# Ten instead of nine gate/up groups of a SwiGLU half-step as seven products of halves

## The chip, the cores and the metric

One core of one Trainium2 chip runs the whole program as a single launch. The metric is the device time in microseconds (us), the median of several runs. TensorE is written PE, its weight loads PEld, VectorE DVE, ScalarE ACT, GpSimd POOL, and SyncE, which issues nearly all transfers, SP.

## What is computed

The reference is one layer of a decoder trunk in float32, on 16 learned meta tokens and 256 tokens of width 2048:

```
h = h + 0.5 * (silu(norm(h) @ w_gate1) * (norm(h) @ w_up1)) @ w_down1        # D_FF = 5632
h = h + mixer(norm(h))            # w_in (2048 x 10248), two attentions, sigmoid gates, w_out
h = h + 0.5 * (silu(norm(h) @ w_gate2) * (norm(h) @ w_up2)) @ w_down2        # D_FF = 5632
return h[:, 16:]
```

## The kernel before

**Units.** Every weight matrix is cut into tiles of 128 x 1024 numbers (512 KB). One tile is a unit: SP loads it (`load`, tile `raw`), ACT rounds it to the faster format (`wh`), DVE takes the rest (`wl = raw - wh`, both in `split_unit`), and PE multiplies with both halves. There are three buffers each of `wh` and `wl`, so the split of a unit waits until PE is done with the unit three before it, and five buffers of `raw` (eight in the second half-step). `ahead(u)` runs ahead of `products(u)`: it issues the load of unit u+5 (u+8 in the second half-step) and the split of unit u+2. The order in which rows stand on an engine is that of the code, moved a little by a scheduler at build time.

**Plain units of the second half-step** multiply both halves of 128 tokens with one tile: 12 products of 512 columns (two halves of the tokens, two rows of 128 weights, and hi*hi, hi*lo, lo*hi). A gate/up pair of 512 features is two blocks of 8 units, 192 products.

**Seven products.** For the groups in `SEVENS` (`Group`) the gate and the up projection of 512 features are taken together as one product of two-by-two blocks with seven instead of eight block products (p1 to p7, Winograd's form). One of the seven takes 4 units of 6 products, so a group has 28 units and 168 products. The order in a group is p1 x4, p5 x4, (p6, p2, p4) x4, p3 x4, p7 x4. p1, p2, p3 read weights, p5, p6, p7 read sums of weights, and p4 reads p6's tile less p2's, which DVE works out (L1135). When the four units of one product are done its bank is evacuated: p1, p5, p6, p4 by an ACT copy, p2 by a DVE add and a silu, p3 by two DVE operations (L1028, L1029), p7 by DVE, silu on ACT and two more on DVE (L1033, L1035, L1036). Then `turn` transposes the result for the down product: eight PE transposes (L440), two ACT copies and two DVE differences.

**Sums of weights.** They don't depend on the tokens. `weight_sums` works them out early, beside the first half-step: for one quarter of a group three loads (tiles `pre`, nine buffers), three DVE subtractions (L1056 to L1060), three stores to DRAM (`sum`). `ahead` takes one of its steps with a pace of 0.94 a unit, from unit 20 to two units before the mixer. The `pre` tiles lie in a pool that `open_attention` closes, at the mixer's first block, and the attention's constants then lie in its place.

**What lies between.** A seven-product unit gives PE half the work of a plain one but costs ACT and DVE the same. So plain units are put between: `eight` holds the units of plain group 1 (16) and of the down projection (88, in parts `PART` of 4 tiles times n each), and ten of them go into every group.

**Mixer.** Its first blocks are q (8 units), forget (2), k (8), v (8) for four heads. PSUM has eight banks; a block of the mixer takes four.

Of the kernel before, what the change touches and what calls it, by code (L numbers as in the profile page):

```python
# [11 lines left out]
ALU = mybir.AluOpType  # L12
# [6 lines left out]
KT = D // P  # L19
# [33 lines left out]
def hybrid_layer(ctx: ExitStack, tc: tile.TileContext, x, meta_tokens, ffn1_norm, ffn1_w_gate, ffn1_w_up,  # L53
# [772 lines left out]

    for g in range(2):
        blocks.append(Block(wi, 0, KT, g * 512, 512, mrhs, NR, fox_evac("q", 4 * g)))
        if g == 0:
            blocks[-1].before = open_attention  # L830
            blocks.append(Block(wi, 0, KT, 3072, 128, mrhs, NT, ev_forget, stacked=8))
        blocks.append(Block(wi, 0, KT, 1024 + g * 512, 512, mrhs, NT, fox_evac("k", 4 * g)))
        blocks.append(Block(wi, 0, KT, 2048 + g * 512, 512, mrhs, NT, fox_evac("v", 4 * g)))
    for c in range(4):
        blocks.append(Block(wi, 0, KT, 6152 + c * 512, 512, mrhs, NR, gate_evac("f", c), True))
# [16 lines left out]

    SEVENS = (2, 3, 4, 5, 6, 7, 8, 9, 10)
    PART = (3, 2, 2, 2, 1, 1)
    acc = {}
    forms = {}

# [10 lines left out]
    def normal_forms():  # L870

        r = norms["ffn2"].r
        yield from residual_by_token()
        yield 1
        for c in range(4):
            for j in range(4):
                t = resid(4 * c + j)[:, :NR]
                act.activation(t, t, AF.Copy, scale=gcol[:, 32 + 4 * c + j:33 + 4 * c + j])
            for j in range(0, 4, 2):
                t = res[c][:, j:j + 2, :NR]  # L880
                dve.tensor_tensor(t, t, r[:, :NR].unsqueeze(1).to_broadcast([P, 2, NR]), op=ALU.mult)
                yield 1

        def x(i, k, c):

            return res[2 * k + c][:, :, i * P:(i + 1) * P]

        def pool():
            return fslot if len(forms) < 4 else slot

        def plain(n, i, k):
            f = pool()
            hi, lo = forms[n] = f([P, 8, P], F32R), f([P, 8, P], F32R)
            for c in range(2):
                split(hi[:, 4 * c:4 * c + 4, :], lo[:, 4 * c:4 * c + 4, :], x(i, k, c))
                yield 2

        def summed(n, t, a, b, op):

            f = pool()  # L900
            hi, lo = forms[n] = f([P, 8, P], F32R), f([P, 8, P], F32R)
            for c in range(2):
                cs = slice(4 * c, 4 * c + 4)
                dve.tensor_tensor(t[:, cs, :], a(c), b(c), op=op)
                yield 1
                split(hi[:, cs, :], lo[:, cs, :], t[:, cs, :])
                yield 2

        yield from plain("a11", 0, 0)
        t = slot([P, 8, P], F32)  # L910
        tq = lambda c: t[:, 4 * c:4 * c + 4, :]
        yield from summed("s1", t, lambda c: x(1, 0, c), lambda c: x(1, 1, c), ALU.add)
        yield from summed("s2", t, tq, lambda c: x(0, 0, c), ALU.subtract)
        yield from plain("a12", 0, 1)
        yield from plain("a22", 1, 1)
        yield from summed("s4", t, lambda c: x(0, 1, c), tq, ALU.subtract)
        t3 = slot([P, 8, P], F32)
        yield from summed("s3", t3, lambda c: x(0, 0, c), lambda c: x(1, 0, c), ALU.subtract)
        while not free["g0"]:
            yield 1  # L920
        yield from plain("a21", 1, 0)

    free = {"g0": False}

    def fslot(shape, dt):
        return ptile(shape, dt, "f", F_BUFS)
# [10 lines left out]

    hs2 = {}

    def plain_group(g):  # L940

        u = {}
        factor = lambda i: norms["ffn2"].rtok[:, i:i + 1] if g == 0 else 1.0

        def ev_gate(i, ps):
            if i == 0:
                u["t"] = slot([P, 2, 512], F32)
            assert norms["ffn2"].done
            act.activation(u["t"][:, i, :], ps[:], AF.Silu, scale=factor(i))

        def ev_up(i, ps):
            s = u["t"][:, i, :]
            if g == 0:
                dve.scalar_tensor_tensor(s, ps[:], factor(i), s, op0=ALU.mult, op1=ALU.mult)
                free["g0"] = i == 1
            else:
                dve.tensor_tensor(s, ps[:], s, op=ALU.mult)
            if i == 1:
                lanes["turn"].append(turn(u["t"], hs2, 4 * g))

        def rhs(kt):
            if g == 0:
                return norms["ffn2"].rhs(kt)
            return [[forms[f"a{i + 1}{kt // 8 + 1}"][m][:, kt % 8, :] for i in range(2)] for m in range(2)]

        return [Block(w[0], 0, KT, g * 512, 512, rhs, NR, ev, True)
                for w, ev in ((ffn2_w_gate, ev_gate), (ffn2_w_up, ev_up))]

    def down_blocks(t0, count, last):
# [120 lines left out]
    units = units_of(blocks)  # L1090
    second = len(units)
    mixer = next(u for u, (b, _, _) in enumerate(units) if b.w is wi)
    units += units_of(plain_group(0))
    seven = [(groups[g], p, u) for g in sorted(groups) for p, u in Group.ORDER]
    starts = [4 * sum(PART[:i]) for i in range(len(PART))]
    down = [down_blocks(t0, 4 * n, t0 + 4 * n == FT) for t0, n in zip(starts, PART)]
    eight = [plain_group(1), *down]
    eight = [u for bs in eight for u in units_of(bs)]
    for g, p, u in seven:
        units.append((g, p, u))  # L1100
        if p == "p2" or p in ("p5", "p3") and u % 2 or p in ("p1", "p7") and u == 1:
            units.append(eight.pop(0))
    units += eight
    raws, halves, banks, newest = {}, {}, {}, []
# [63 lines left out]
    def products(u):  # L1168
# [12 lines left out]
        for j in range(outs):  # L1181
# [10 lines left out]
            for i in range(0 if wide else n):  # L1192
                x = b.rhs(k0 + i)
                first, last = k0 + i == 0, k0 + i == b.kts - 1
                if b.by_token:
                    xh, xl = (x[0][j], x[1][j]) if isinstance(x, list) else (x[:, 0, cs], x[:, 1, cs])
                    terms = ((ps[:], xh, wh[:, i, :]), (ps[:], xh, wl[:, i, :]), (ps[:], xl, wh[:, i, :]))
                elif b.stacked:
                    terms = tuple((ps[:, :b.n], wh[:, i, cs], x[:, m, :b.n]) for m in range(2))
                else:  # L1200
                    o, xh, xl = ps[:, :b.n], x[:, 0, :b.n], x[:, 1, :b.n]
                    terms = ((o, wh[:, i, cs], xh), (o, wh[:, i, cs], xl), (o, wl[:, i, cs], xh))
                for m, (o, a, c) in enumerate(terms):
                    pe.matmul(o, a, c, start=first and m == 0, stop=last and m == len(terms) - 1)  # L1204
# [24 lines left out]

    def ahead(u):  # L1230
        nonlocal loaded, done, sums_due
        if SUMS_FROM <= u < mixer - 2:
            sums_due += SUMS_PACE
            while sums_due >= 1:
                sums_due -= 1
                next(ahead_sums, None)
        while loaded < min(len(units), u + (LOAD_AHEAD if u < second else SECOND_AHEAD)):
            load(loaded)
            loaded += 1
        while done < min(len(units), u + 1 + SPLIT_AHEAD):  # L1240
            split_unit(done)
            done += 1
# [69 lines left out]
```

## Time and profile before

| | |
|---|---|
| median of three runs | 2206.59 us (2205.45 to 2206.94) |
| profiled execution | 2207.63 us, span from first to last instruction 2205.9 us |
| PE busy | 2199.1 us, 13716 products and transposes |
| DVE busy | 1603.0 us, 73% of the span |
| ACT busy | 1170.5 us, 53% of the span |
| moved by DMA | 554.09 MB, mean 251 GB/s |

The profiled execution lies 1.04 us over the median of the runs and 1.7 us over its own span. Busy time of PE includes pipelined matmuls, whose ends are modelled, so idle time is better read from the starts of matmuls.

### The profile page before, as it was taken

To read this page: it belongs to the slowest core of one execution; us is meant where nothing else is said; L and a number is where in the kernel's file an instruction comes from. 1 tells how busy PE (TensorE), PEld (TensorE's weight loads), DVE (VectorE), ACT (ScalarE), POOL (GpSimd) and SP (SyncE) were. 2 spreads that over 40 slices of the span, in tenths; PEclk is the share of its full clock that TensorE was granted. 3 is DMA by queue.
4 is the path that set the end of the run, shared out by engine and by line. 5 is a ranking of instruction groups with operands and counts; after the bars stand their busy time and mean duration, and the time that the engine had idled before them with its cause. 6 is when DMAs were issued, how large, how long until landed. Compare 5 with 4: busy or idle time off the path is not lost.

```text
span 2205.9 us, 34841 instructions
## 1 busy us (share of the span) xinstructions
PE 2199.1 (100%) x13716; PEld 1997.0 (91%) x13716; DVE 1603.0 (73%) x1944; ACT 1170.5 (53%) x1467; POOL 42.1 (2%) x113
## 2 busy tenths in 40 slices
PE   9999999999999999999999999999999999999999
PEld 9999999999999999998899988888888888888887
DVE  6676666667766765889556665667888888888886
ACT  6344433334443454656445565458666666666663
POOL 0000000000000001110000000000000000000000
PEclk9999999999999999999999999999999999999999
DMA  7899999999999966555655456555788777888774
GB/s 225 281 330 324 340 318 348 343 338 333 347 336 340 323 202 191 164 166 158 190 183 164 146 156 201 179 187 163 241 272 269 261 262 260 275 272 270 258 260 171
DMA packets 262021, 554.09 MB, mean 251 GB/s; under 512 B 17289, under 2 KB 22241, under 8 KB 261857
## 3 DMA queue, kind: packets, MB, share of 16 engines
q1 hardware_dynamic: 259776, 548.34, 75.2%
q8 instruction: 107, 1.75, 0.3%
q10 hardware_dynamic: 1472, 2.37, 0.3%
q0 software_dynamic: 608, 1.16, 0.2%
q14 instruction: 58, 0.47, 0.1%
HBM read 493.07 MB, written 58.73 MB: 250 GB/s over the span
## 4 chain that ended last, share of the span: by engine, by line
PE 99%; DMA 0%; DVE 0%; SPq 0%; issue 0%; DVEq 0%; ACT 0%
PE acc L1204 72%; PE acc L1003 16%; PE acc L1187 5%; PE acc L1190 3%; PE aux L727 1%; PE aux L600 1%; PE aux L440 1%; PE aux L588 0%; PE aux L698 0%; DMA v<-in_meta_tokens_dram 0%; PE acc L1165 0%; PE aux L866 0%; PE aux L340 0%; PE aux L677 0%; PE aux L678 0%; PE aux L640 0%
## 5 line engine op out<-in xcount | busy, mean ns | idle before, releaser
L190 ACT ACTIVATE wh<-raw 128x1024 fp32r<-128x1024 f32 (+1 forms) x609 | 644.4, 1059 | 779.1 <-PE acc L1204 621.9
L191 DVE TENSOR_TENSOR wl<-raw,wh 128x1024 fp32r<-128x1024 f32 (+1 forms) x609 | 743.1, 1222 | 432.3 <-ACT wh L190 428.3
L1204 PE MATMUL acc<-v,wh 128*128 128x272 f32 x5264 | 991.4, 288 | 0.0
L1204 PEld LDWEIGHTS acc<-v,wh 128*128 128x128 f32 x5264 | 827.4, 189 | 0.1
L1204 PE MATMUL acc<-v,wl 128*128 128x272 f32 x2616 | 753.5, 289 | 0.4 <-DVE wl L191 0.4
L1204 PE MATMUL acc<-wh,v 128*128 128x512 f32 x1664 | 540.8, 392 | 0.0
L1204 PEld LDWEIGHTS acc<-v,wl 128*128 128x128 f32 x2616 | 490.8, 188 | 0.8 <-DVE wl L191 0.6
L1204 PEld LDWEIGHTS acc<-wh,v 128*128 128x128 f32 x1664 | 312.5, 188 | 64.6
L1136 DVE TENSOR_TENSOR wl<-raw,wh 128x1024 fp32r<-128x1024 f32 x252 | 305.1, 1221 | 41.5 <-ACT wh L1130 33.4
L1130 ACT ACTIVATE wh<-raw 128x1024 fp32r<-128x1024 f32 x252 | 266.5, 1060 | 124.3 <-PE acc L1204 75.4
L1204 PE MATMUL acc<-wl,v 128*128 128x512 f32 x832 | 327.8, 394 | 0.0
L1204 PEld LDWEIGHTS acc<-wl,v 128*128 128x128 f32 x832 | 156.2, 188 | 38.8 <-DVE wl L191 7.1
L1003 PE MATMUL acc<-wh,f 128*128 128x512 f32 x576 | 191.3, 393 | 0.0
L1187 PE MATMUL acc<-v,wh 128*128 128x512 f32 x512 | 160.6, 395 | 0.0
L1003 PE MATMUL acc<-wh,v 128*128 128x512 f32 x432 | 143.3, 389 | 0.0
L1003 PEld LDWEIGHTS acc<-wh,f 128*128 128x128 f32 x576 | 108.2, 188 | 22.5
L1190 PEld LDWEIGHTS acc<-v,wl 128*128 128x128 f32 x512 | 96.1, 188 | 22.0
L1003 PE MATMUL acc<-wl,f 128*128 128x512 f32 x288 | 113.2, 393 | 0.0
L1190 PE MATMUL acc<-v,wl 128*128 128x256 f32 x512 | 101.3, 279 | 0.0
L1003 PEld LDWEIGHTS acc<-wh,v 128*128 128x128 f32 x432 | 81.1, 188 | 16.9
L1003 PE MATMUL acc<-wl,v 128*128 128x512 f32 x216 | 84.0, 389 | 0.0
L1187 PEld LDWEIGHTS acc<-v,wh 128*128 128x128 f32 x512 | 78.4, 188 | 0.2
(264 smaller groups left out, 1378.5 us busy)
## 6 DMA issues: line engine op xcount, KB each, us to landing
raw<-in_ffn_w_down_dram SPq DMA_DIRECT2D x176, 512.0 KB, 5.4
raw<-in_ffn_w_gate_dram SPq DMA_DIRECT2D x175, 512.0 KB, 5.2
raw<-in_w_in_dram SPq DMA_DIRECT2D x162, 512.0 KB, 3.7
raw<-in_ffn_w_up_dram SPq DMA_DIRECT2D x140, 512.0 KB, 5.1
sum<-pre SPq DMA_DIRECT2D x108, 512.0 KB, 6.5
raw<-sum SPq DMA_DIRECT2D x108, 512.0 KB, 4.6
pre<-in_ffn_w_up_dram SPq DMA_DIRECT2D x72, 512.0 KB, 6.9
pre<-in_ffn_w_gate_dram SPq DMA_DIRECT2D x36, 512.0 KB, 6.8
```

Source lines behind the costliest of these rows:

```text
L190: act.activation(hi, src, AF.Copy)
L191: dve.tensor_tensor(lo, src, hi.bitcast(F32), op=ALU.subtract)
L440: pe.transpose(p[:, (2 * j + i) * P:(2 * j + i + 1) * P], u[:, i, c:c + P], ident[:])
L600: pe.matmul(po[:, :NR], a[:, ks], b[:, i * NR:(i + 1) * NR], start=n == 0, stop=n == 6)
L727: pe.matmul(o, a, b, start=start, stop=stop, skip_group_check=True)
L1003: pe.matmul(ps[:], a[:, kt, :], b[:, i, :], start=fresh and kt == 0 and m == 0, stop=kt == 7 and m == 2, skip_group_check=True)
L1130: act.activation(wh[:], raw[:], AF.Copy)
L1136: dve.tensor_tensor(wl[:], raw[:], wh[:].bitcast(F32), op=ALU.subtract)
L1187: pe.matmul(ps[:].rearrange("p (a t) -> p a t", a=2), wh[:, i, cs], x[:, :, :NR], start=k0 + i == 0, stop=False, skip_group_check=True)
L1190: pe.matmul(ps[:, :NR], wl[:, i, cs], x[:, 0, :NR], start=False, stop=k0 + i == b.kts - 1, skip_group_check=True)
L1204: pe.matmul(o, a, c, start=first and m == 0, stop=last and m == len(terms) - 1)
```

## The change

Gate/up group 1, until now computed as eight products between the others' units, becomes the first of ten groups by seven products. `plain_group(1)` and the form of the tokens that only it needed (`a21`) go; only group 0 stays plain (`first_group`). Its twelve more sums of weights need 24 more steps of `weight_sums`, 12 loads and 12 stores: the steps go on at 1.5 a unit into the mixer's first 15 units, and the forget block, which opens the attention, moves behind q and k. With 88 instead of 104 plain units to put between, groups 1 and 2 get four each (after p2), groups 3 to 9 eight (after p2, and after every second unit of p5 and p3), group 10 twelve. The down projection is cut into seven parts instead of six.

```
-        if g == 0:
-            blocks[-1].before = open_attention
-            blocks.append(Block(wi, 0, KT, 3072, 128, mrhs, NT, ev_forget, stacked=8))
-        blocks.append(Block(wi, 0, KT, 1024 + g * 512, 512, mrhs, NT, fox_evac("k", 4 * g)))
+        blocks.append(Block(wi, 0, KT, 1024 + g * 512, 512, mrhs, NT, fox_evac("k", 4 * g)))
+        if g == 0:
+            blocks.append(Block(wi, 0, KT, 3072, 128, mrhs, NT, ev_forget, stacked=8, before=open_attention))
...
-    SEVENS = (2, 3, 4, 5, 6, 7, 8, 9, 10)
-    PART = (3, 2, 2, 2, 1, 1)
+    SEVENS = (1, 2, 3, 4, 5, 6, 7, 8, 9, 10)
+    PART = (1, 2, 2, 2, 2, 1, 1)
...
-        while not free["g0"]:
-            yield 1
-        yield from plain("a21", 1, 0)
...
-        if p == "p2" or p in ("p5", "p3") and u % 2 or p in ("p1", "p7") and u == 1:
+        if p == "p2" or u % 2 and (g.g > 2 and p in ("p5", "p3") or g.g == SEVENS[-1] and p in ("p1", "p7")):
             units.append(eight.pop(0))
...
-        if SUMS_FROM <= u < mixer - 2:
-            sums_due += SUMS_PACE
+        if SUMS_FROM <= u < mixer + 15:
+            sums_due += SUMS_PACE if u < mixer - 2 else 1.5
```

How the change moves instructions is shown at three places. First DVE where one group ends and the next begins (after L1033, which is L1019 in the changed file: the evacuation of p7). Before, the rows are these; the L191 rows are splits of plain units, the L1136 rows those of seven-product units:

```order
L191 TENSOR_TENSOR wl_2868_18479<-raw_2846_18386,wh_2867_18478 128x1024
L1136 TENSOR_TENSOR wl_2871_18491<-raw_2849_18398,wh_2870_18490 128x1024
L1136 TENSOR_TENSOR wl_2874_18503<-raw_2852_18410,wh_2873_18502 128x1024
L1136 TENSOR_TENSOR wl_2877_18521<-raw_2855_18430,wh_2876_18520 128x1024
L1136 TENSOR_TENSOR wl_2880_18533<-raw_2858_18442,wh_2879_18532 128x1024
L1033 TENSOR_TENSOR v_2775_18067<-acc_2760_17998,v_2775_18067 128x512
L1035 TENSOR_TENSOR v_2776_18068<-v_2776_18068,acc_2760_17998 128x512
L191 TENSOR_TENSOR wl_2883_18549<-raw_2861_18456,wh_2882_18548 128x1024
L1036 TENSOR_TENSOR v_2776_18068<-v_2776_18068,v_2775_18067 128x512
L1136 TENSOR_TENSOR wl_2887_18562<-raw_2866_18476,wh_2886_18561 128x1024
```

In the changed kernel the same place (end of group 3, start of group 4; L1121 is the split of a seven-product unit) reads:

```order
L1121 TENSOR_TENSOR wl_2839_18300<-raw_2819_18209,wh_2838_18299 128x1024
L1121 TENSOR_TENSOR wl_2842_18312<-raw_2822_18221,wh_2841_18311 128x1024
L1121 TENSOR_TENSOR wl_2845_18324<-raw_2825_18239,wh_2844_18323 128x1024
L1019 TENSOR_TENSOR v_2741_17868<-acc_2731_17825,v_2741_17868 128x512
L1021 TENSOR_TENSOR v_2742_17869<-v_2742_17869,acc_2731_17825 128x512
L1121 TENSOR_TENSOR wl_2848_18340<-raw_2828_18251,wh_2847_18339 128x1024
L1022 TENSOR_TENSOR v_2742_17869<-v_2742_17869,v_2741_17868 128x512
L1121 TENSOR_TENSOR wl_2852_18353<-raw_2831_18265,wh_2851_18352 128x1024
```

The split behind the two evacuations was that of a plain unit, and is now that of the third unit of p1.

Second, DVE in group 1 of the changed kernel, from the last unit of p5 (`wl_2538`) over p6 and p2 to the first plain unit between and p4 (L1120 is p6's tile less p2's; the two rows on `aux` are the `turn` of group 0):

```order
L1121 TENSOR_TENSOR wl_2538_17001<-raw_2513_16907,wh_2537_17000 128x1024
L191 TENSOR_TENSOR v_2535_16995<-aux_2534_16990,v_2535_16995 128x2x256
L1121 TENSOR_TENSOR wl_2541_17013<-raw_2516_16927,wh_2540_17012 128x1024
L1121 TENSOR_TENSOR wl_2545_17031<-raw_2520_16940,wh_2544_17030 128x1024
L191 TENSOR_TENSOR v_2543_17027<-aux_2542_17022,v_2543_17027 128x2x256
L1120 TENSOR_TENSOR raw_2516_16927<-raw_2516_16927,raw_2520_16940 128x1024
L191 TENSOR_TENSOR wl_2548_17045<-raw_2523_16952,wh_2547_17044 128x1024
L1121 TENSOR_TENSOR wl_2551_17057<-raw_2516_16927,wh_2550_17056 128x1024
```

Before, two plain units stood between p5's units and one between p1's, so a turn's two differences came in three units' more time.

Third, SP at the mixer's first blocks (the tiles of `w_in`). Before, from the last store of a sum, it reads:

```order
L1052 DMA sum10_2_3_9135<-pre_1132_8789 128x1024
L1121 DMA raw_1173_9137<-in_ffn1_w_down_dram 128x2x512
L1121 DMA raw_1176_9167<-in_ffn1_w_down_dram 128x2x512
L1121 DMA raw_1179_9197<-in_ffn1_w_down_dram 128x2x512
L1121 DMA raw_1182_9227<-in_w_in_dram 128x2x512
L1121 DMA raw_1185_9257<-in_w_in_dram 128x2x512
```

and goes on with loads of `w_in` alone. In the changed kernel, from the fifth load of `w_in` on:

```order
L1106 DMA raw_1197_9339<-in_w_in_dram 128x2x512
L1057 DMA pre_1200_9369<-in_ffn2_w_gate_dram 128x2x512
L1057 DMA pre_1201_9371<-in_ffn2_w_up_dram 128x2x512
L1106 DMA raw_1202_9374<-in_w_in_dram 128x2x512
L1057 DMA pre_1211_9430<-in_ffn2_w_up_dram 128x2x512
L1106 DMA raw_1212_9433<-in_w_in_dram 128x2x512
L1038 DMA sum10_0_1_9459<-pre_1179_9174 128x1024
L1038 DMA sum10_1_1_9461<-pre_1183_9206 128x1024
L1106 DMA raw_1219_9463<-in_w_in_dram 128x2x512
L1038 DMA sum10_2_1_9485<-pre_1187_9239 128x1024
L1106 DMA raw_1222_9488<-in_w_in_dram 128x2x512
```

Between one load of `w_in` and the next there are now one or two transfers of the sums, up to the sixteenth load.

## Rows read from the trace of the kernel before

**Rows 1.** The page: busy time by engine, granted clock in 40 slices.
```profile
PE 2199.1 (100%) x13716; PEld 1997.0 (91%) x13716; DVE 1603.0 (73%) x1944; ACT 1170.5 (53%) x1467; POOL 42.1 (2%) x113
...
PEclk9999999999999999999999999999999999999999
```
**Rows 2.** Waits of PE, then PEld: us in total, times, longest us.
```profile
PE acc L1204 <- DVE wl L191: 0.4, 1, 0.4
...
PEld acc L1204 <- DVE wl L191: 9.4, 29, 0.6
```
**Rows 3.** The chain that ended last, in order of time: start us, us, what.
```profile
1758.16 5.44 PE acc L1003 x24
...
1825.19 5.44 PE acc L1003 x24
```
**Rows 4.** Windows: busy us (instructions) by engine, granted clock, DMA share, GB/s.
```profile
705.00:745.00 40.00, 40.00 (x321) 40.00 (x320) 26.40 (x30) 17.13 (x22) 0.00 (x0) 1.00 0.98 355
797.00:846.00 49.00, 49.00 (x343) 46.28 (x342) 32.88 (x60) 27.36 (x40) 3.52 (x13) 1.00 0.62 184
...
1771.50:1838.50 67.00, 67.00 (x298) 54.46 (x297) 57.21 (x55) 43.81 (x47) 0.00 (x0) 1.00 0.80 267
```
**Rows 5.** DVE groups by line, 1771.5 to 1838.5 us: busy us, mean ns.
```profile
L1136 DVE TENSOR_TENSOR wl<-raw,wh 128x1024 fp32r<-128x1024 f32 x28 | 33.9, 1221 | 3.9 <-ACT wh L1130 3.0
...
L1135 DVE TENSOR_TENSOR raw<-raw,raw 128x1024 f32<-128x1024 f32 x4 | 4.9, 1222 | 0.1
L933 DVE SCALAR_TENSOR_TENSOR v<-acc,v 128x512 f32<-128x512 f32 x4 | 2.6, 681 | 0.0
```
**Rows 6.** Timeline of DVE, ACT and PE where a group ends: start us, us.
```profile
1826.32 2.59 DVE L1136 TENSOR_TENSOR wl<-raw,wh 128x1024 fp32r<-128x1024 f32 x2 [0.30 <-ACT wh L1130]
1828.83 0.68 DVE L1033 TENSOR_TENSOR v<-acc,v 128x512 f32<-128x512 f32 x1
1829.42 0.68 DVE L1035 TENSOR_TENSOR v<-v,acc 128x512 f32<-128x512 f32 x1
1830.02 1.22 DVE L191 TENSOR_TENSOR wl<-raw,wh 128x1024 fp32r<-128x1024 f32 x1
1831.16 0.68 DVE L1036 TENSOR_TENSOR v<-v,v 128x512 f32<-128x512 f32 x1
...
1838.84 1.23 DVE L191 TENSOR_TENSOR wl<-raw,wh 128x1024 fp32r<-128x1024 f32 x1 [0.26 <-ACT wh L190]
...
1826.59 1.06 ACT L1130 ACTIVATE wh<-raw 128x1024 fp32r<-128x1024 f32 x1 [0.30 <-PE acc L1003]
...
1827.75 0.39 PE L1003 MATMUL acc<-wh,f 128*128 128x512 f32 x1
...
1830.47 0.62 PE L1204 MATMUL acc<-wh,v 128*128 128x512 f32 x2
...
1839.78 0.39 PE L1204 MATMUL acc<-wh,v 128*128 128x512 f32 x1
1840.12 0.50 PE L1204 MATMUL acc<-wl,v 128*128 128x512 f32 x1
1840.46 0.62 PE L1204 MATMUL acc<-wh,v 128*128 128x512 f32 x2
```
**Rows 7.** The page's DMA issues: count, KB each, median us to landing.
```profile
raw<-in_w_in_dram SPq DMA_DIRECT2D x162, 512.0 KB, 3.7
...
sum<-pre SPq DMA_DIRECT2D x108, 512.0 KB, 6.5
```
**Rows 8.** Timeline at the mixer's start: a tile's buffer freed, loaded, split.
```profile
800.06 1.23 DVE L191 TENSOR_TENSOR wl<-raw,wh 128x1024 fp32r<-128x1024 f32 x1 [1.79 <-ACT wh L190]
...
801.31 16.00 SPq L1121 DMA_DIRECT2D raw<-in_w_in_dram  x6
...
813.91 1.04 ACT L190 ACTIVATE wh<-raw 128x1024 fp32r<-128x1024 f32 x1
```

More of the change, by code (lines that the diff above doesn't have):

```diff
@@ L918, in normal_forms @@
         yield from summed("s3", t3, lambda c: x(0, 0, c), lambda c: x(1, 0, c), ALU.subtract)
-        while not free["g0"]:
-            yield 1
-        yield from plain("a21", 1, 0)
-    free = {"g0": False}
     def fslot(shape, dt):
@@ L938, in hybrid_layer, with first_group @@
     hs2 = {}
-    def plain_group(g):
+    def first_group():
         u = {}
-        factor = lambda i: norms["ffn2"].rtok[:, i:i + 1] if g == 0 else 1.0
+        factor = lambda i: norms["ffn2"].rtok[:, i:i + 1]
         def ev_gate(i, ps):
@@ L952, in ev_up @@
             s = u["t"][:, i, :]
-            if g == 0:
[L954 to L957, printed above, removed]
-            if i == 1:
[L959 to L966, printed above, removed]
+            dve.scalar_tensor_tensor(s, ps[:], factor(i), s, op0=ALU.mult, op1=ALU.mult)
+            if i == 1:
+                lanes["turn"].append(turn(u["t"], hs2, 0))
+        rhs = lambda kt: norms["ffn2"].rhs(kt)
+        return [Block(w[0], 0, KT, 0, 512, rhs, NR, ev, True)
                 for w, ev in ((ffn2_w_gate, ev_gate), (ffn2_w_up, ev_up))]
@@ L1092, in hybrid_layer @@
     mixer = next(u for u, (b, _, _) in enumerate(units) if b.w is wi)
-    units += units_of(plain_group(0))
+    units += units_of(first_group())
     seven = [(groups[g], p, u) for g in sorted(groups) for p, u in Group.ORDER]
@@ L1096, in hybrid_layer @@
     down = [down_blocks(t0, 4 * n, t0 + 4 * n == FT) for t0, n in zip(starts, PART)]
-    eight = [plain_group(1), *down]
-    eight = [u for bs in eight for u in units_of(bs)]
+    eight = [u for bs in down for u in units_of(bs)]
     for g, p, u in seven:
         units.append((g, p, u))
-        if p == "p2" or p in ("p5", "p3") and u % 2 or p in ("p1", "p7") and u == 1:
+        if p == "p2" or u % 2 and (g.g > 2 and p in ("p5", "p3") or g.g == SEVENS[-1] and p in ("p1", "p7")):
             units.append(eight.pop(0))
@@ L1195, in products @@
                 if b.by_token:
-                    xh, xl = (x[0][j], x[1][j]) if isinstance(x, list) else (x[:, 0, cs], x[:, 1, cs])
+                    xh, xl = x[:, 0, cs], x[:, 1, cs]
                     terms = ((ps[:], xh, wh[:, i, :]), (ps[:], xh, wl[:, i, :]), (ps[:], xl, wh[:, i, :]))
```

## The prediction

> **What bounds the kernel now.** I began with busy time by engine: PE is busy 2199.1 of 2205.9 us, DVE 73%, ACT 53%, and the granted clock stands at nine tenths or more in each slice, 1.00 in the windows, the 2.4 GHz level [rows 1, 4]. The waits say the same: after the first 60 us PE itself waits once, 0.4 us, and its weight loads wait 9.4 us in 29 pieces, for late splits [rows 2]. So a product taken away is time taken away, as long as DVE's splits stay ahead. The chain gives the price of a product: 24 in 5.44 us, 0.2267 us each, and the same row comes back 67.03 us later [rows 3]. That is one group: 28 units of 6 and 10 of 12 are 288 products, 65.29 us; the other 1.74 us are eight transposes and small waits. What such a wait costs is seen at 1839.78: the split ends at 1838.84 + 1.23 = 1840.07, its product was due 0.23 after the start, at 1840.01, and comes at 1840.12; the next again needs 0.34 instead of 0.23 [rows 6]. A split 0.06 us late costs 0.22 us. Each group has three such places, 0.66 us: this one, one at 1830.47 and one 19 us earlier, where ACT copies p4.
>
> **What is removed.** Plain group 1 has 16 units of 12 products, 192; as seven products it has 168. The down projection and the transposes stay. 24 x 0.2267 = 5.44 us less [rows 3]. This is the most that can be won, 0.25%; 0.2%, 4.4 us, is about what a measurement of this kernel can tell from no change.
>
> **How far DVE keeps up.** DVE's operations start 0.60 us apart at 512 columns (1828.83, 1829.42, 1830.02) and 1.14 apart at 1024 (1830.02, 1831.16), though each lasts 0.68 and 1.22 [rows 5, 6]. A group with k plain units needs on DVE (28 + 4 + k) x 1.14 for splits and p4's differences, 8 x 0.60 for evacuations and turn, and 0.60 for each evacuation of a down block; PE needs 38.1 + 2.72k. Before, k = 10: 55.7 against 65.3 us, 85%, as the window shows (57.21 of 67.0) [rows 4]. After, k = 8 in groups 3 to 9: 45.6 + 4.8 + 2.4 = 52.8 against 59.9. In groups 1 and 2, k = 4: 41.0 + 4.8 + 2.4 = 48.3 against 49.0, 98%. So DVE fits as a sum. But lead can't be saved up, for there are three buffers: ACT starts when the unit three before is done, at 1826.59, 0.20 us after the boundary (1827.75 less a unit of 1.36), and DVE ends at 1826.32 + 2.59 = 1828.91, 2.52 us after it [rows 6]. The rest is needed two units and a product later, 2 x 1.36 + 0.23 = 2.95: among seven-product units there is 0.38 us to spare (0.05 is the hand-over), and an extra operation of 0.60 is made good by 0.22 us per unit. A plain unit between gives 1.36 more.
>
> The VectorE: DVE Perf Modes page of the Trainium skill ("The DRAIN you can't avoid") says that a DVE operation doesn't start until the one before has emptied the pipe. The rows contradict it here, with starts 0.08 us earlier than ends; by that rule groups 1 and 2 would be DVE-bound, which is the third rival below.
>
> **Ends of groups 3 to 9.** When p7 ends at 1827.75, DVE is busy until 1828.91, then come the two evacuations, and the next split ends at 1831.24, 3.49 us after the boundary: 0.54 late [rows 6]. Today that split is a plain unit's, and PE's order puts products and a transpose ahead of it, so only 0.22 is lost. In the changed order it is the split of p1's third unit, whose second product directly follows its first: I take 0.54 + 0.05 + 0.11 = 0.7 us. Behind it waits L1022 with the next split, but there PE's order has a product and two transposes ahead, which cover it. The place of 1839.78 should go, since the turn's differences now come later, next to a plain unit, and ACT's stays. So 0.92 for 0.66 us, 0.26 x 7 = 1.8 us. Bounds: 0, if the order hides it as today; 5.7, if L1022's split costs 0.38 more and no place goes (1.47 for 0.66).
>
> **Groups 1 and 2.** Here p1, p5, p3 and p7 have no plain unit between. (a) At the first p2 a difference of the turn, p4's subtraction and the split stand in a row, 0.60 + 1.14 + 1.14 = 2.88 us against 0.38 + 1.36: 1.14 late; PE's order has two (group 2: three) products ahead, which leaves about 0.8 and 0.5 with the hand-over. (b) p3's two evacuations stand before successive splits: lead 0.38 + 0.22 - 0.60 = 0, then -0.38, with one product ahead: about 0.5. (c) p7's: 0.7. (d) ACT's copy: 0.22. That is 2.2 and 1.9, 4.1 us. Before, the work from group 0's end to that of group 2, a little over one and a half groups at three places each, lost some five times 0.22 us, 1.1. I take +3.0 us; bounds 0 (all hidden) and 5 (PE's order helps nowhere).
>
> **The last sums in the mixer.** Twelve more subtractions, 13.7 us on DVE, stand where DVE is busy 32.88 of 49.0 us: hidden; each stands on DVE about five units behind the issue of the tiles that it reads, so it waits for them only if they take over some 14 us. The transfers are the question. From the fifth to the sixteenth load of `w_in` SP issues 15 transfers of sums and 11 loads, 13.6 MB. Six loads take 16.00 us to issue [rows 8], so 11 take about 32 us by 2.9 us a unit; in the first half-step, where the engines are busy to 0.98, they move 355 GB/s [rows 4], which makes 38 us. The arrears grow to 6 us by the twelfth load and shrink over the next three, which come alone. In that saturated stage a sum lands 6.5 us after its issue, a load of `w_in` alone after 3.7 [rows 7]; I expect up to 13. A buffer freed by the split of 800.06 is loaded at 801.31 and split at 813.91, 12.6 us later [rows 8]; with units of 2.9 us the split leads PE by 2 x 2.9 - 2.52 = 3.3 us more. Only a landing over 15.9 us stops PE. The cover is about 3 us; without it the 6 us of arrears are lost. I take 0.3 us, bounds 0 and 6.
>
> The HBM Reference page of the Trainium skill says that a core streaming alone reaches about 425 GB/s, at which 13.6 MB would take 32 us and no arrears would form. The row has 355 GB/s at a share of 0.98, for loads and stores mixed; no run here shows more, and the sum goes by the row.
>
> The other moves cost nothing. Forget now stands before v instead of before k; its cumulated sums are wanted by the first head's attention, a whole v block of some 24 us later. The attention's constants wait until the last stores have landed; these are issued with the load of a unit five ahead, some 14 us before. If they are later, DVE stands before the constants and PE loses what goes beyond 3.3 us of lead. At the end 13 instead of 14 plain units follow p7, and the last turn is still covered by five units of 2.72 us before the last down part needs it.
>
> **The sum.** The profiled execution took 2207.63 us (span 2205.9 and 1.7 around it). 2207.63 - 5.44 + 1.8 + 3.0 + 0.3 = 2207.3. It lies 1.04 over the median of the runs, so I predict 2206.3: the products won are spent on late splits.
>
> **The rivals.**
> 1. The waits don't come: PE's order at build time hides them, as it hides nearly all today, and the extra is under 1 us: 2206.59 - 5.44 = 2201.2 to 2202. For it: DVE's sum fits in each group. Against: at p7 the products put ahead stand one unit too late.
> 2. Slower by the mixer: the loads of `w_in` land over 15.9 us after their issue, and PE waits for the arrears. The price is up to 6 us, 2212. For it: 440 GB/s asked for, 355 seen. Against: 3 us of cover, and the three loads that come alone.
> 3. DVE is the bound in groups 1 and 2. With full durations, 1.22 and 0.68, a group takes 36 x 1.22 + 12 x 0.68 = 52.1 us against 49.0 and 0.9 for transposes, 2.2 too much, twice: 4.4 us more, 2210.7. For it: 98% use. Against: starts 1.14 apart.
>
> **How the numbers follow.** The forecast, extra waits of 2 to 8 us, gets 0.65 and by itself reaches from 2203 to 2209.5; rival 1 gets 0.13, rival 2 0.12, rival 3 0.09, and 0.01 is left. Faster by over 4.4 us is rival 1 and a rest, 0.14. Slower by over 4.4 us needs most of rival 2's price, or rival 3 with the upper bound at the group ends: 0.17. The range, 2202 to 2211, takes in the forecast's own and about half of each rival.
>
> **What would show it.** PE has 24 fewer products and no other. The row of 24 products where a group ends repeats after 59.9 us and about 1.9 more in groups 3 to 9. At p1's third unit the second product comes about 0.7 us late, behind DVE's split. Groups 1 and 2 each lose about 2 us. In the mixer the sums land after up to 13 us, and ACT never waits for a load. The prediction is wrong if PE's starts show less than 2 us or more than 8 us of new waits in the second half-step, or ACT waits for `raw` in the mixer.

## The result, and the profile after

The changed kernel takes 2213.76 us (median of six, 2212.97 to 2214.33) beside 2206.62 for the kernel before: ratio 1.0033, 95% interval 1.0022 to 1.0043. It is 7.1 us slower, where 2206.3 was forecast and 2211 was the upper end. The profiled execution has a span of 2212.6 us, 6.7 more than before.

The chain that ended last, by engine, on the page of the kernel before:

```profile
PE 99%; DMA 0%; DVE 0%; SPq 0%; issue 0%; DVEq 0%; ACT 0%
```

The page of the changed kernel: busy time by engine, the same chain, and the transfers of the sums (count, KB, median us to landing).

```profile
PE 2200.4 (99%) x13692; PEld 1992.5 (90%) x13692; DVE 1635.2 (74%) x1982; ACT 1183.2 (53%) x1481; POOL 43.7 (2%) x113
...
PE 94%; DVE 3%; issue 1%; ACT 1%; DMA 0%; SPq 0%; DVEq 0%; ACTq 0%
...
sum<-pre SPq DMA_DIRECT2D x120, 512.0 KB, 6.6
```

PE has 24 instructions fewer [rows 1], as it should. But PE is now 94% of the chain that ended last, where it was 99%, and DVE, ACT and issue have nearly all the rest. What PE and its weight loads wait for, from 60 us on (us in total, times, longest us), says with what:

```profile
PE acc L989 <- DVE wl L1121: 3.4, 8, 0.4
PE acc L1189 <- DVE wl L191: 1.3, 1, 1.3
PE acc L1189 <- ACT wh L190: 0.8, 1, 0.8
...
PEld acc L989 <- DVE wl L1121: 13.9, 31, 0.9
PEld acc L1189 <- DVE wl L191: 7.5, 21, 1.5
```

Before, splits of plain units and of the other blocks cost PE 0.4 us and its weight loads 9.4 [rows 2]; those of seven-product units (L1136 there) cost the weight loads little, and PE nothing:

```profile
PEld acc L1003 <- DVE wl L1136: 1.3, 7, 0.2
```

Two things are new: eight waits of products on the splits of seven-product units (L1121), and two at a single place in the mixer (L1189), of 0.8 and 1.3 us.

**Where the time went.** The rows of waits count a wait of PE and of its weight loads apart, so a ledger is better: for each two products that follow each other, the distance of their starts less the bare pitch of their form (0.227 us at 512 columns, 0.125 at 272, 0.119 at 256, 0.109 for a transpose), added up by stage. Its borders are fixed times, so a few tenths may stand on the wrong side of one. In us:

| stage | before | after | difference |
|---|---|---|---|
| first half-step (60 to 797) | 3.9 | 3.3 | -0.7 |
| the mixer's first blocks (797 to 850) | 1.2 | 4.9 | +3.7 |
| rest of the mixer, group 0 (850 to 1560) | 6.2 | 6.6 | +0.4 |
| groups 1 and 2 (1560 to 1690) | 1.7 | 4.4 | +2.6 |
| groups 3 to 10 (1690 to 2110) | 5.2 | 10.9 | +5.7 |
| the end (2110 to 2215) | 0.3 | 0.7 | +0.4 |

That is 12.1 us more, and 5.44 less for the products: +6.7, which is the difference of the spans. Two of the rows carry the error, the mixer and groups 3 to 10.

The timeline of the changed kernel at both places (start us, us, what it was released by): first the end of q's block in the mixer on ACT, DVE and PE, then the end of a group on DVE, ACT and PE.

```profile
824.69 1.06 ACT L190 ACTIVATE wh<-raw 128x1024 fp32r<-128x1024 f32 x1 [1.71 <-PE acc L1172]
832.10 0.94 ACT L1192 ACTIVATE sum<-acc 128x256 f32<-128x256 f32 x3 [6.35 <-PE acc L1175]
832.91 1.07 ACT L190 ACTIVATE wh<-raw 128x1024 fp32r<-128x1024 f32 x1
...
832.52 0.42 DVE L1193 TENSOR_TENSOR sum<-sum,acc 128x256 f32<-128x256 f32 x1 [4.33 <-ACT sum L1192]
832.86 1.22 DVE L1044 TENSOR_TENSOR pre<-pre,pre 128x1024 f32<-128x1024 f32 x1
...
835.33 1.22 DVE L191 TENSOR_TENSOR wl<-raw,wh 128x1024 fp32r<-128x1024 f32 x1
...
834.03 1.26 PE L1189 MATMUL acc<-v,wh 128*128 128x272 f32 x8 [0.80 <-ACT wh L190]
836.59 0.60 PE L1189 MATMUL acc<-v,wl 128*128 128x272 f32 x1 [1.30 <-DVE wl L191]
...
1853.41 0.69 DVE L1019 TENSOR_TENSOR v<-acc,v 128x512 f32<-128x512 f32 x1
1854.01 0.68 DVE L1021 TENSOR_TENSOR v<-v,acc 128x512 f32<-128x512 f32 x1
1854.61 1.22 DVE L1121 TENSOR_TENSOR wl<-raw,wh 128x1024 fp32r<-128x1024 f32 x1
...
1860.77 1.23 DVE L191 TENSOR_TENSOR wl<-raw,wh 128x1024 fp32r<-128x1024 f32 x1 [0.94 <-ACT wh L190]
...
1859.19 0.60 ACT L996 ACTIVATE v<-acc 128x512 f32<-128x512 f32 x1 [0.77 <-PE acc L989]
1859.69 1.05 ACT L190 ACTIVATE wh<-raw 128x1024 fp32r<-128x1024 f32 x1
...
1854.83 0.61 PE L989 MATMUL acc<-wh,f 128*128 128x512 f32 x2
1855.88 0.50 PE L989 MATMUL acc<-wl,f 128*128 128x512 f32 x1 [0.43 <-DVE wl L1121]
1856.22 0.64 PE L989 MATMUL acc<-wh,f 128*128 128x512 f32 x2
...
1861.63 0.48 PE L1189 MATMUL acc<-wh,v 128*128 128x512 f32 x1
1862.05 0.50 PE L1189 MATMUL acc<-wl,v 128*128 128x512 f32 x1
```

**The mixer.** From 825.75 to 832.10 ACT does nothing. It waits for q's last products, because three copies of q's evacuation (L1192) stand next in its row; the split of k's first unit (832.91) stands behind them, and PE, done with q's starts at 832.95, has nothing to multiply until 834.03. On DVE the same: the split of 835.33 stands behind five operations of q's evacuation and a subtraction of sums (832.86), 2.8 us in all. In the code that split comes before q's evacuation, since `ahead` issues it a unit earlier; the order of the built program is another. By the starts of its products PE loses 0.96 and 1.46 us, and then the windows (us, busy us by engine, granted clock, DMA share, GB/s) show a third loss:

```profile
797.00:832.00 35.00, 35.00 (x232) 32.34 (x231) 25.52 (x37) 17.27 (x24) 1.59 (x4) 1.00 1.03 384
...
832.00:834.00 2.00, 1.23 (x9) 0.94 (x7) 1.48 (x3) 1.88 (x4) 0.00 (x0) 1.00 0.77 298
834.00:836.50 2.50, 1.26 (x8) 1.05 (x8) 2.50 (x7) 2.00 (x3) 0.00 (x0) 1.00 0.11 43
836.50:840.00 3.50, 3.41 (x15) 3.41 (x16) 3.50 (x7) 0.28 (x1) 0.00 (x0) 0.51 0.54 126
```

After the two waits, from 836.5 to 840 us, the granted clock is 0.51, the 1.2 GHz level, and a product of 272 columns takes 0.227 instead of 0.125 us; the thirteen of them from 836.99 on lose 1.3 us. The transfers, which I had feared, were in time: the mixer's start moved 384 GB/s at a share of 1.03, above the 355 at 0.98 [rows 4] that I took for the most there is, and ACT never waits for `raw` there.

**Ends of groups.** The third unit of p1 gets its second product 0.59 us late, at 1855.88, and the next again needs 0.11 more: 0.70, as forecast. But a plain unit after it waits as well (1861.63 to 1862.05, 0.42 instead of 0.23, 0.30 in all), and p7's third unit does (0.32). The two have other reasons than p7's evacuation. The plain unit's split on DVE (1860.77) follows 0.94 us of waiting for ACT, where the copy that evacuates p1 (L996, 1859.19) had to wait for p1's last product and stood ahead of that unit's split (1859.69). Before, ACT's split for the same place (1839.78) stood behind p1's copy and one of the turn's:

```profile
1836.77 0.60 ACT L1010 ACTIVATE v<-acc 128x512 f32<-128x512 f32 x1 [0.28 <-PE acc L1003]
1837.27 0.60 ACT L190 ACTIVATE v<-aux 128x512 fp32r<-128x512 f32 x1
```

The split of p7's third unit stands on DVE behind p3's second operation (L1015) and the two evacuations of a block of the down projection (L927), which ends with the plain unit just before p7; PE's product comes right behind it:

```profile
1846.64 0.68 DVE L1015 TENSOR_TENSOR v<-v,v 128x512 f32<-128x512 f32 x1
1847.24 1.28 DVE L927 SCALAR_TENSOR_TENSOR v<-acc,v 128x512 f32<-128x512 f32 x2
1848.44 3.48 DVE L1121 TENSOR_TENSOR wl<-raw,wh 128x1024 fp32r<-128x1024 f32 x3
...
1849.71 0.50 PE L989 MATMUL acc<-wl,v 128*128 128x512 f32 x1
```

In the chain of the changed kernel the first evacuation of p7, above at 1853.41, comes again a group later:

```profile
1915.82 0.68 DVE v L1019
```

So a group takes 62.41 us. Its products need 264 x 0.2267 = 59.85 and its eight transposes 0.87, so 1.7 are lost. Before it was 67.03 [rows 3] for 65.29 and 0.87: 0.9 lost. That is 0.8 a group, where I had 0.26.

### The profile page after: what moved, and what is told of

Same layout as the page of the kernel before. It is cut to its first block, busy times and chain, and to the rows that moved or that the text cites. A ratio compares the mean times of both kernels' runs of the same rounds, so it can differ in the third digit from the quotient of the medians.

```text
span 2212.6 us, 34895 instructions
## 1 busy us (share of the span) xinstructions
PE 2200.4 (99%) x13692; PEld 1992.5 (90%) x13692; DVE 1635.2 (74%) x1982; ACT 1183.2 (53%) x1481; POOL 43.7 (2%) x113
## 4 chain that ended last, share of the span: by engine, by line
PE 94%; DVE 3%; issue 1%; ACT 1%; DMA 0%; SPq 0%; DVEq 0%; ACTq 0%
PE acc L1189 69%; PE acc L989 14%; PE acc L1172 5%; PE acc L1175 3%; DVE wl L1121 2%; PE aux L727 1%; ACT wh L1115 1%; PE aux L600 1%; PE aux L440 1%; DVE v L1014 0%; DVE v L1019 0%; PE aux L588 0%; PE aux L698 0%; DVE v L927 0%; DVE v L1021 0%
## 5 line engine op out<-in xcount | busy, mean ns | idle before, releaser
L191 DVE TENSOR_TENSOR wl<-raw,wh 128x1024 fp32r<-128x1024 f32 (+1 forms) x593 | 723.6, 1222 | 418.8 <-ACT wh L190 415.3
L190 ACT ACTIVATE wh<-raw 128x1024 fp32r<-128x1024 f32 (+1 forms) x593 | 627.3, 1059 | 744.8 <-PE acc L1189 617.9
L1189 PE MATMUL acc<-v,wh 128*128 128x272 f32 x5264 | 991.2, 289 | 0.8 <-ACT wh L190 0.8
L1189 PEld LDWEIGHTS acc<-v,wh 128*128 128x128 f32 x5264 | 827.5, 189 | 1.2 <-ACT wh L190 1.0
L1189 PE MATMUL acc<-v,wl 128*128 128x272 f32 x2616 | 752.4, 289 | 1.3 <-DVE wl L191 1.3
L1189 PE MATMUL acc<-wh,v 128*128 128x512 f32 x1600 | 521.0, 393 | 0.1
L1189 PEld LDWEIGHTS acc<-v,wl 128*128 128x128 f32 x2616 | 491.0, 188 | 1.8 <-DVE wl L191 1.7
L1115 ACT ACTIVATE wh<-raw 128x1024 fp32r<-128x1024 f32 x280 | 295.2, 1060 | 132.2 <-PE acc L989 58.5
L1189 PEld LDWEIGHTS acc<-wh,v 128*128 128x128 f32 x1600 | 300.4, 188 | 62.1 <-ACT wh L190 0.5
L1121 DVE TENSOR_TENSOR wl<-raw,wh 128x1024 fp32r<-128x1024 f32 x280 | 336.0, 1221 | 25.9 <-ACT wh L1115 22.1
L1189 PE MATMUL acc<-wl,v 128*128 128x512 f32 x800 | 314.9, 394 | 0.0
L989 PE MATMUL acc<-wh,f 128*128 128x512 f32 x640 | 208.4, 391 | 0.0
L1189 PEld LDWEIGHTS acc<-wl,v 128*128 128x128 f32 x800 | 150.3, 188 | 36.3 <-DVE wl L191 6.0
L989 PEld LDWEIGHTS acc<-wh,f 128*128 128x128 f32 x640 | 120.2, 188 | 24.3
L989 PE MATMUL acc<-wl,f 128*128 128x512 f32 x320 | 126.8, 396 | 3.4 <-DVE wl L1121 3.4
```

The lines of the kernel that those rows point to most:

```text
L190: act.activation(hi, src, AF.Copy)
L191: dve.tensor_tensor(lo, src, hi.bitcast(F32), op=ALU.subtract)
L989: pe.matmul(ps[:], a[:, kt, :], b[:, i, :], start=fresh and kt == 0 and m == 0, stop=kt == 7 and m == 2, skip_group_check=True)
L1115: act.activation(wh[:], raw[:], AF.Copy)
L1121: dve.tensor_tensor(wl[:], raw[:], wh[:].bitcast(F32), op=ALU.subtract)
```

## The experiments

My theory after the result had two independent parts. A: the mixer's loss is a matter of order on ACT and DVE at q's end. C: the loss of groups 3 to 9 comes because p7 and p1 have no plain unit beside them any more, so that evacuations and the turn meet units that give PE half the work. The rivals: B, the last sums hold up the splits by themselves; D, DVE's lead is too short everywhere, and a wait only moves when plain units are moved. Ratios are to the kernel before, with 95% intervals.

**1. The splits ahead of q's evacuation.** `pins` holds the last split on ACT and on DVE; the copy and the add that evacuate q, or another block with two sets of 272 columns, are issued behind it.

```
+        pins[:] = [act.activation(wh[:], raw[:], AF.Copy).ins,
+                   dve.tensor_tensor(wl[:], raw[:], wh[:].bitcast(F32), op=ALU.subtract).ins]
...
-                act.activation(t[:], ps[:, NR:2 * NR], AF.Copy)
-                dve.tensor_tensor(t[:], t[:], ps[:, :NR], op=ALU.add)
+                with tc.issue_after(pins[0]):
+                    act.activation(t[:], ps[:, NR:2 * NR], AF.Copy)
+                with tc.issue_after(pins[1]):
+                    dve.tensor_tensor(t[:], t[:], ps[:, :NR], op=ALU.add)
```

> The changed kernel; only the order on ACT and DVE at the ends of the blocks with two sets of 272 columns (q among them) is held to that of the code: the splits of k's first two units stand ahead of q's evacuation, not behind three of its copies. The last sums stay in the mixer. Theory A (the 3.7 us lost in the mixer are a matter of order: k's first split, whose tile had long landed, is queued behind copies that wait for q's end): the wait of 0.96 and that of 1.46 us at q's end go, 3.7 us less, 2210.0 us. Rival B (the transfers or the subtractions of the last sums hold the splits up): the splits wait in their new place for raw, or the slow pace comes behind a subtraction, and the time stays within 1 us of 2213.8.

Measured: 2210.4 us, 1.0018 (1.0009 to 1.0027), 3.4 less. ACT's timeline at the same place, and the window of the mixer's first blocks:

```profile
826.51 1.06 ACT L1133 ACTIVATE wh<-raw 128x1024 fp32r<-128x1024 f32 x1 [1.72 <-PE acc L1174]
829.29 1.06 ACT L1133 ACTIVATE wh<-raw 128x1024 fp32r<-128x1024 f32 x1 [1.72 <-PE acc L1174]
831.13 0.94 ACT L1195 ACTIVATE sum<-acc 128x256 f32<-128x256 f32 x3 [0.79 <-PE acc L1177]
```

```profile
797.00:846.00 49.00, 49.00 (x343) 46.25 (x342) 39.44 (x54) 25.78 (x35) 2.57 (x4) 1.00 1.03 371
```

k's first two splits (826.51, 829.29) wait for nothing but a free buffer, so their tiles had landed. PE has no gap, the clock stays at 1.00, and the ledger of that stage falls from 4.9 to 0.8. Theory A holds, and B falls.

**2. Without the last sums.** The mixer has neither the transfers nor the subtractions of group 10's sums; that group reads those of group 9.

```
-        work = [(group, u) for group in groups.values() for u in range(4)]
+        work = [(group, u) for group in groups.values() if group.g < 10 for u in range(4)]
...
+    groups[10].sums = groups[9].sums
```

> The changed kernel without the sums of group 10 (its products read those of group 9, so its share of the output is not the reference's): the mixer issues no transfer and no subtraction of sums, the order of its blocks stays that of the change. Theory A: the order at q's end falls back to the splits first by itself, 3.7 us less, 2210.0 us, the same as with the order held by hand. If it is clearly below that (2208 or less), the last sums cost something besides the order; if it stays near 2213.8, the moved forget block costs the time and not the sums.

Measured: 2210.32 us, 1.0015 (1.0006 to 1.0024). Without transfers of sums between the loads, the built program has k's splits ahead of q's evacuation by itself, and the stage's ledger is 0.8. So the subtractions and transfers in the mixer cost nothing that shows but the order, and the forget block's move, which run 2 keeps, nothing at all. Why the order turns, perhaps because k's tile is reckoned late at build time, was not tried.

**3 and 4. Other places for the eight plain units of groups 3 to 9.** In run 3 after p2, p5's odd units, and the second unit of p1 and p7; in run 4 after p2 and the second unit of p1, p5, p3 and p7.

```
-        if p == "p2" or u % 2 and (g.g > 2 and p in ("p5", "p3") or g.g == SEVENS[-1] and p in ("p1", "p7")):
+        if p == "p2" or g.g > 2 and (p == "p5" and u % 2 or p in ("p1", "p7") and u == 1
+                                     or g.g == SEVENS[-1] and p in ("p1", "p7", "p3") and u % 2):
...
+        if p == "p2" or g.g > 2 and p != "p4" and p != "p6" and (u == 1 or g.g == SEVENS[-1] and u == 3):
```

> The changed kernel with the eight plain units of groups 3 to 9 put elsewhere: after p2 (4) and p5's odd units (2) as now, but after the second unit of p7 and of p1 instead of p3's odd ones. Theory C (each group of 3 to 9 loses 1.5 us because the evacuation of p7 and the turn's differences now meet units of half the products): the waits at p7's third and p1's third unit fall to 0.2 us, those beside p3 rise by 0.2, about 0.6 us less a group, 2209.5 us. Rival D (DVE has too little lead all over with eight plain units, and a wait only moves): within 1 us of 2213.8.

> As the run before, but the plain units of groups 3 to 9 stand after p2 (4) and after the second unit of p1, p5, p3 and p7 (one each). Theory C: every evacuation has one plain unit near, the waits fall from 1.5 to about 0.8 us a group, 2209 us. Rival D: within 1 us of 2213.8. If the wait behind p5's units, where the turn's differences stand, grows to more than 0.5 us, the second plain unit there is worth more than one beside p3.

Measured: run 3 2206.65 us, 0.9997 (0.9988 to 1.0007); run 4 2208.92, 1.0011 (1.0002 to 1.0020). The weight loads' waits in groups 3 to 10 (1690 to 2110 us) in run 3 are

```profile
PEld acc L989 <- DVE wl L1122: 3.9, 14, 0.4
PEld acc L1190 <- DVE wl L191: 3.9, 17, 0.3
```

where the changed kernel has 9.8 and 4.2, and PE itself waits no more there. The ledger of the stage falls from 10.9 to 4.8 (run 3) and 7.1 (run 4). Theory C holds, and gave more than I had expected of run 3: at the end of a group no single distance is more than 0.11 us over its pitch. Moving the plain units also moves the ends of the down blocks away from p3's evacuation, so for p7's third unit it was not shown which of the two helped. Run 4 keeps a wait of 0.21 us on ACT's split in each group. D is wrong: the waits don't merely move.

**5 and 6. Both cures, and one plain unit moved from group 1's last p2 to group 2's p1.**

```
-        if p == "p2" or g.g > 2 and (p == "p5" and u % 2 or p in ("p1", "p7") and u == 1
+        if p == "p2" and (g.g, u) != (1, 3) or (g.g, p, u) == (2, "p1", 1) or g.g > 2 and (p == "p5" and u % 2 or p in ("p1", "p7") and u == 1
...
```

> The changed kernel with both cures: the splits of k's first units held ahead of q's evacuation, and the plain units of groups 3 to 9 after p2, p5's odd units and the second units of p7 and p1. If the two losses are independent, their gains add: 2213.8 - 3.4 - 7.1 = 2203.3 us, ratio to the kernel before 0.998. If they share a cause (a state of the order that either cure resets), the sum is less, 2206 or more.

> The run before with one plain unit moved in the first two groups: from behind the last p2 of group 1 to behind the second unit of p1 in group 2, where the evacuation of group 1's p7 makes the split 0.6 us late. Theory C: that wait goes (0.5 us less), and the last p4 of group 1 gets a wait of at most that; 2203.0, no more than 0.5 us from the run before either way. If p2's plain units are what carries p4's subtraction, it is slower by 1 us or more.

Measured: 2202.64 us, 0.9983 (0.9974 to 0.9992), and 2202.77, 0.9982 (0.9973 to 0.9991). The gains of 1 and 3 add up; in groups 1 and 2 the moved unit bought one wait with another.

**7 and 11. Four buffers.** The argument behind the prediction was that DVE has room as a sum, but that three buffers don't let it save up lead. In the second half-step every fourth unit gets a `wh` and `wl` of its own, which two of the eight buffers of `raw` pay for. Run 7 also issues splits three units ahead, run 11 two, as before.

```
-SECOND_AHEAD = 9
+SECOND_AHEAD = 8
...
-        if loaded >= second and loaded % 8 >= RAW_BUFS:
-            return ptile(shape, F32, "raw", 8 - RAW_BUFS)
+        if loaded >= second and loaded % 6 >= RAW_BUFS:
+            return ptile(shape, F32, "raw", 6 - RAW_BUFS)
...
+    def half_tiles(u, shape):
+        if u >= second and u % 4 == 3:
+            return [ptile(shape, F32R, t) for t in ("wh", "wl")]
+        return [wp.tile(shape, F32R, tag=t, name=name(t)) for t in ("wh", "wl")]
...
-        while done < min(len(units), u + 1 + SPLIT_AHEAD):
+        while done < min(len(units), u + 1 + SPLIT_AHEAD + (u > second)):
```

> The changed kernel with its own order of units, but in the second half-step a fourth buffer of wh and of wl (two buffers of raw fewer, six, and loads one unit less ahead), and splits run three units ahead. Theory E (DVE has room as a sum in every group, and the waits come only because three buffers don't let lead be saved): the waits of the second half-step fall from 15 us to about 6, what the kernel before has there, 2205 us, with the mixer's 3.7 still in. Rival F (DVE is the bound in groups 1 and 2, at 98% as a sum): their 4.4 us stay, 2207. Rival G (six buffers of raw are too few): ACT waits for raw, and the time is 2210 or more.

> The changed kernel with the fourth buffers, but the splits still issued two units ahead in the code. If it is the buffer that lets a split start a unit earlier: 2198, within 1.5 us of the run with a lead of three. If it is the place of the split ahead of the evacuations on DVE that counts: the waits at the ends of groups 3 to 9 stay, 7 x 0.7 = 5 us more, 2203.

Measured: run 7 2197.82 us, 0.9958 (0.9945 to 0.9970); run 11 2198.68, 0.9963 (0.9950 to 0.9975). The ledger of groups 3 to 10 falls from 10.9 to 0.0 in both, that of groups 1 and 2 from 4.4 to 1.4 and 1.1: more than I had expected, since the waits that the kernel before has go as well. It is the buffer that does it, not the lead in the code. Theory E holds and F falls: DVE is not the bound in groups 1 and 2.

**8 and 9. Four buffers with the cures.** Run 8 has both, run 9 only the order at q's end.

> The fourth buffers of the run before on top of both cures. By theory E at most 2203.3 less the group waits that are left there (4.8 us in groups 3 to 9 and 3.7 in 1 and 2, of which about 4 are bound to transposes): 2199 to 2201.5 us. If the waits that are left are none of the splits', it stays at 2203.3.

> The changed kernel with its own order of units, the fourth buffers, and the splits of k's first units held ahead of q's evacuation. With four buffers, moving plain units no longer helped (the run with both and the other places gave 2197.0, with 2.9 us of waits in groups 3 to 9 where the changed kernel's own places leave none), and the mixer's wait is untouched by the buffers: 2197.8 - 2.6 = 2195.2 us. If the other places were right after all, it is 2197 or more.

Measured: 2196.97 us, 0.9955 (0.9942 to 0.9967), and 2195.12, 0.9946 (0.9934 to 0.9959). Run 8 doesn't add up: its groups 3 to 10 have 2.9 us in the ledger again, and ACT waits 48 us there for loads, against 8 in the whole second half-step of run 9. As the loads went in these runs, the change's own places are the better ones; the buffers of `raw` went round unevenly in both (see run 10), and run 8 was not tried with that mended.

**10, 12 and 13. What the change is worth once splits have lead.** The kernel before with the fourth buffers (run 10), then with the sixth buffer of `raw` given to every sixth tile that is loaded (run 12), and run 9 with the same (run 13).

```
-        if loaded >= second and loaded % 8 >= RAW_BUFS:
-            return ptile(shape, F32, "raw", 8 - RAW_BUFS)
+        if loaded >= second:
+            turns[0] += 1
+            if turns[0] % 6 == 5:
+                return ptile(shape, F32, "raw")
```

> The kernel before, nine groups by seven products, with the fourth buffers of wh and wl (and six of raw) in its second half-step, nothing else. Its second half-step has 7.2 us over the bare pitch of its products; by theory E all but about 0.5 of that go, 2200.0 us. Then the change, with both of its losses cured, is worth 2200.0 - 2195.2 = 4.8 us, nearly the whole 5.44 of its 24 products. If the kernel before gains as much as the changed one did (16 us, 2191), the change itself is a loss that no order of its units cures; if it gains nothing (2206), the buffers help the changed kernel alone.

> The kernel before with the fourth buffers again; the sixth buffer of raw is now taken by every sixth tile that is loaded (the run before counted p4's units too, which load nothing, so that the sixth buffer stood idle through parts of a group, and ACT waited 34.7 us for loads of the down projection in ten places). Theory G (the run before gained nothing because raw came late): those waits shrink, and 2206.5 falls to about 2200 to 2202. If ACT waits as long as there, six buffers are too few where a plain unit follows p7 and p1, and the time stays at 2206. If ACT doesn't wait for raw and the time stays at 2206, theory E is wrong for the kernel before.

> The best version so far (four buffers, splits of k held ahead) with the sixth buffer of raw taken by every sixth loaded tile. Its groups have no late split left, so theory E gives no more to win: 2195.1, within 1 us. If the even turn of the buffers takes one from where it was needed (p6's tile is held until p4), it is slower by 1 to 3 us, with ACT waiting for raw.

Measured: run 10 2206.52 us, 1.0000 (0.9991 to 1.0009), no gain; run 12 2199.16, 0.9966 (0.9954 to 0.9978); run 13 2195.05, 0.9945 (0.9933 to 0.9958). ACT's waits for loads in the second half-step, in run 10:

```profile
ACT wh L190 <- DMA raw<-in_ffn_w_down_dram: 34.7, 10, 4.4
ACT wh L190 <- DMA raw<-in_ffn_w_gate_dram: 3.6, 1, 3.6
```

and in run 12, where only 0.5 more is for a sum:

```profile
ACT wh L1139 <- DMA raw<-in_ffn_w_up_dram: 1.8, 2, 1.2
```

In run 10 the splits were late because the tiles were: `loaded` counts p4's units too, which load nothing, so the sixth buffer went round unevenly. With that mended the kernel before loses nothing in its groups either. Between runs 12 and 13, side by side, lie 4.1 us by the medians: that is the change without its waits (and with q's end in order), three quarters of its 5.44. The ledgers of their profiled executions differ by 0.4 us, which would leave 5.0 of it; single runs of either kernel scatter over about 3 us. A group of run 13 at its end, DVE and PE:

```profile
1779.04 0.68 DVE L1019 TENSOR_TENSOR v<-acc,v 128x512 f32<-128x512 f32 x1
1779.64 0.68 DVE L1021 TENSOR_TENSOR v<-v,acc 128x512 f32<-128x512 f32 x1
...
1839.83 0.68 DVE L1019 TENSOR_TENSOR v<-acc,v 128x512 f32<-128x512 f32 x1
...
1840.56 0.61 PE L989 MATMUL acc<-wh,f 128*128 128x512 f32 x2
1841.02 0.39 PE L989 MATMUL acc<-wl,f 128*128 128x512 f32 x1
1841.24 0.61 PE L989 MATMUL acc<-wh,f 128*128 128x512 f32 x2
```

The group takes 60.79 us, the 59.85 of its products, the 0.87 of its transposes and 0.07 more; where the changed kernel had its 0.70, products start 0.22 apart. Run 13's windows, each nearly one of groups 1 and 2, and the chain that ended last on its page:

```profile
1548.00:1597.00 49.00, 49.00 (x222) 40.56 (x221) 46.66 (x49) 35.01 (x40) 0.00 (x0) 1.00 0.77 252
1597.00:1646.00 49.00, 49.00 (x221) 40.39 (x220) 48.09 (x48) 36.09 (x40) 0.00 (x0) 1.00 0.84 293
```

```profile
PE 99%; DMA 0%; DVE 0%; SPq 0%; issue 0%; DVEq 0%
```

## Why the prediction was wrong

- **Products: 5.44 us less.** Right; PE has 24 instructions fewer, and with the waits gone the change brings 4.1 by the medians.
- **Groups 1 and 2: 3.0 us.** Nearly right, 2.6 by the ledger.
- **Ends of groups 3 to 9, "0.92 for 0.66", 1.8 us: this step failed in size.** By the periods it is 1.7 for 0.9, by the ledger 5.7 us in all. The wait at p1's third unit was right to 0.01 us. Wrong was the sentence "The place of 1839.78 should go, since the turn's differences now come later, next to a plain unit": it stayed, at 1861.63, and cost 0.30 us instead of 0.22. The differences did not make it: the row at 1838.84 has DVE waiting 0.26 us for ACT's split [rows 6], and in the changed kernel, with the turn out of the way, that split still stands behind p1's copy. And p7's third unit, which before had a plain unit just ahead of it, became a new place of 0.32 us; the evacuations of the down blocks, which come there with p3's, were in DVE's sum but in none of the places. That the total equals the upper bound of 5.7 is luck: the bound took L1022's split to be late, which cost nothing, and its terms add up to 1.52 a group and 6.0 us, not 1.47 and 5.7. The plain reading of the new order would have served better: each unit that lost its plain neighbour waits. Run 3 gave p7 and p1 theirs back, and the waits went.
- **The last sums in the mixer, 0.3 us: this step failed in its mechanism.** I asked only whether transfers would be late. They were not; the longest of a sum or its source there took 9.4 us, not up to 13. The 3.7 us are ACT's and DVE's order at q's end (runs 1 and 2), with a fall of the clock behind it. For that stage the order had been read on SP, for its transfers, and not on ACT. The second rival came within 2 us of the measured time (2212 for 2213.8) by luck, with a wrong cause (and its 13.6 MB in 32 us are 425 GB/s, not 440).
- **"The other moves cost nothing".** Right for the forget block (run 2).
- **"Lead can't be saved up, for there are three buffers".** Right, and the best use of it was not in the change: a fourth buffer takes away what both kernels lose (runs 7, 11, 12).
- **Rival 3.** Wrong: in run 13 groups 1 and 2 have 0.5 us in the ledger together, and group 2 takes 50.3 us there (p7's first evacuations stand at 1607.39 and 1657.64), so DVE does in that time what at full durations would take 52.1. In the rows of run 13 above, an operation of 512 columns starts 0.60 us after the one before, which lasts 0.68. The rule of the Trainium skill (VectorE: DVE Perf Modes, "The DRAIN you can't avoid") by which that rival went does not show in these rows; but the prediction gave only half of it, for the same section says that a next operation that is not held starts earlier, so the rows need not contradict the page.

The sum of the errors: 3.4 for the mixer, 3.9 for the group ends, -0.4 for groups 1 and 2, which is 6.9; forecast and measured time lie 7.5 us apart, and the rest lies in the other stages and in the profiled executions' distance to the medians. The prediction's own sign of being wrong is met too: the second half-step has 8.7 us of new waits, more than 8.

## What to carry to other kernels

Before work is moved into a stage with room, look on every engine, the idlest too, at what stands between the last instruction of one block and the first that the next block needs: one copy that waits for the end of a block, ahead of a split whose data are there, costs the whole lead. When fillers get fewer, put those that are left where the bound engine's partner has its bursts (evacuations), and check the place that each removed filler had covered. And when waits are short and spread while the engine that is late has room as a sum, a buffer more can be worth more than any order that was tried: 16 us for the changed kernel, three times what the change was meant to bring, and 7.9 for the kernel before. But look at what pays for it: in the kernel before it brought nothing until the buffers of `raw` that were left went round evenly (runs 10 and 12).

## What the runs showed of the hardware

- The two waits in the mixer, 0.96 and 1.46 us, are the same to 0.005 us in the changed kernel and in runs 3, 4, 7 and 11. In the changed kernel and in runs 3 and 4 the granted clock then fell to about half for 3 us and cost 1.5 more (the ledger from 830 to 846 us has 4.1 in the changed kernel against 2.6 in run 7); in runs 7 and 11 it stayed at 1.00. The windows of run 7:

```profile
832.00:836.50 4.50, 2.40 (x17) 1.98 (x17) 4.50 (x7) 3.26 (x5) 0.00 (x0) 1.00 0.16 61
836.50:840.00 3.50, 3.50 (x30) 3.50 (x30) 3.50 (x7) 1.06 (x1) 0.00 (x0) 1.00 0.81 253
```

  In the changed kernel and in run 7 PE was busy a little over half the time from 832 to 836.5 us (1.23 + 1.26 and 2.40 of 4.5 us). The same stall cost 2.6 or 4.1 us; what decides was not found.
- One core moved 384 GB/s over 35 us, loads and stores mixed, where I had taken 355 for its limit. The HBM Reference page of the Trainium skill (Specifications (TRN2)), which has about 425 GB/s for a core alone, was the better guide: ACT waited for no load there.
